# Projecting the memory's V 512 columns wide in a two-layer decoder trunk, with other fill pieces and another order of the cross-attention

## The chip, the core and the metric

The kernel runs on one core of a Trainium2 chip. Its time is the device time of one execution in microseconds; the time of a version is the median of several executions. TensorE multiplies matrices, ScalarE and VectorE evict and convert, GpSimd does some elementwise work, SyncE issues the transfers.

## What is computed

Two post-norm decoder layers on 256 tokens of width 1024, all in float32. Each layer has a token-mixing attention, a cross-attention into 256 memory tokens and a gated feed-forward part, each followed by a residual layer norm. The change touches the cross-attention:

```python
def memory_cross_attn(x, memn, wq, wkv, wo):
    q = (x @ wq).reshape(B, S, XA_HEADS, XA_DH)             # 4 heads of 256
    k, v = jnp.split(memn @ wkv, 2, axis=-1)
    s = jnp.einsum('bshd,bmhd->bhsm', q, k) * (XA_DH ** -0.5)
    p = jax.nn.softmax(s, axis=-1)
    o = jnp.einsum('bhsm,bmhd->bshd', p, v).reshape(B, S, XA_HEADS * XA_DH)
    return o @ wo
```

`memn` is the normed memory. It is the same for both layers and depends on no token, so K and V of a layer can be projected long before its cross-attention.

## The kernel before

**Products in three parts.** Each float32 operand is split into a high half (ScalarE copies it to the matmul's type) and a low half (VectorE subtracts), and a product is high x high, high x low and low x high, added up in one PSUM bank. Weights pass through `piece`: a load of up to 128 x 1024 into one of 4 raw buffers, then L130 (ScalarE, high) and L131 (VectorE, low) into one of 6 buffers each. `wmat` cuts a matrix into such pieces: four row blocks of 256 columns, or two of 512.

**Tokens.** There are two tiles of 128 tokens. After each norm `transposed` turns a tile with eight TensorE transposes into two banks, and ScalarE (L250) and VectorE (L251) evict the high and low half into `xT`. `mm_tr` (L177 to L179) has the weights stationary and streams both tiles, 256 columns; `mm_nat` (L169 to L171) has the tokens stationary and streams the weights' columns.

**Norms.** `layer_norm` takes a tile through VectorE (residual L217, mean L227), ScalarE (squares L228), VectorE (L229), GpSimd (reciprocal root L209) and VectorE again (L239, L240). The first tile's norm runs while TensorE still multiplies for the second.

**Fill pieces.** While the second tile's norm runs, TensorE gets work that wants no tokens: `fill(kv, n)` takes n pieces from `kv.work`, the four K pieces, and then from `kv.vwork`, the V pieces in the order `vord`. A K piece is 48 matmuls of 256 columns. A V piece before the change is a quarter of V's columns: 48 matmuls of 256 columns into one bank, first tile 0 of the memory, then tile 1. What V pieces are left when the cross-attention comes to them are projected there (`xa_v`) and split straight into the operand `vx`; those that were done as fill have been copied to a plain `kv.v` and are only split there.

For layer 0 three K pieces are placed by name in the attention's list of steps, and `lnfill` (3) pieces follow the first norm: K3, V1, V0. V2 and V3 are left to the cross-attention. For layer 1, `CFG[0]['fill']` (2) pieces stand behind the second norm of layer 0 (K0, K1), `CFG[1]['fill']` (2) behind the third norm of layer 0 (K2, K3), and `lnfill` (2) behind the first norm of layer 1 (V0, V1); V2 and V3 are left to the cross-attention.

**The order.** The program order of the steps is written out in two lists per layer, `attn` and `cross`. A list scheduler places the instructions on the engines by that order and by when it expects their inputs, so an engine may take a later step's instruction while an earlier one still waits. On the chip each engine then runs its instructions in the order so made. PSUM has eight banks in two pools of four, `a` and `b`; fill pieces and the accumulators of the output projections use pool `a`.

In the cross-attention's list, `q0` to `q3` project the queries, `qk0` to `qk3` make scores and softmax, `v0` to `v3` prepare V, and `av0` to `av3` transpose the probabilities and multiply them with V.

Of the kernel before, what the change touches and what calls it, by code (L numbers as in the profile page):

```python
# [13 lines left out]
AF = mybir.ActivationFunctionType  # L14
# [5 lines left out]
D = 1024  # L20
S = 256
DEPTH = 2
NT = S // P
KD = D // P
# [29 lines left out]
def consts():  # L54
# [24 lines left out]


CFG = [
    {'attn': 'kc nq1 nq0 par k cmp v mem tab qk0 cq qk1 cps ckv cmt fill av0 qk2 av1 av2 ch qk3 kr mq2 mq0 fill mkv par2 mq1 mq3 av3 mqk2 mqk3 mqk0 mqk1 mav0 mav1 fill mav3 mav2', 'cross': 'q2 q3 q0 q1 qk2 qk3 qk0 v0 v2 v1 qk1 av2 av0 v3 av1 av3', 'ev': [[[0, 0], [1, 0]], [1, 1]], 'fill': 2, 'lnfill': 3, 'vord': (1, 0, 3, 2), 'xt': ('q1', 'k1', 'q0'), 'opt': {'B': 0, 'M': 1, 'C': 0, 'N00': 0, 'N01': 0, 'N10': 0, 'N11': 0, 'N20': 0, 'N21': 0, 'R0': 1, 'R1': 1, 'K': 0, 'H': 0, 'X0': 0, 'X1': 1}, 'lnact': {'in': [0, 1], 'mem': [1, 0], '1': [1, 1], '2': [0, 0], '3': [0, 1]}, 'last': 5, 'natural': 0, 'bank': {'acc0': 'a', 'acc1': 'a', 'fill': 'a', 'proj': 'a', 'pv': 'a', 'mpv': 'b', 'mlav': 'b', 'xpv': 'b', 'nat': 'a', 'lnt': 'b', 'par': 'a', 'projt': 'a', 'cmp': 'b', 'cmps': 'b', 'cmpt': 'a', 'pt': 'b', 'qk': 'b', 'cht': 'a', 'mla': 'a', 'mqk': 'b', 'xq': 'a', 'xqk': 'a', 'xpt': 'b', 'up': 'b'}},
    {'attn': 'kc nq1 nq0 k cmp v qk0 cps ckv cmt av0 qk1 qk2 cq av1 ch av2 qk3 kr mq0 mkv mq3 mq1 av3 mqk0 mq2 mqk1 mqk3 mav0 mav3 mqk2 mav1 mav2', 'cross': 'q0 q1 q2 q3 qk0 v0 v2 av0 v1 qk1 qk2 qk3 v3 av2 av3 av1', 'ev': [[[0, 0], [0, 0]], [1, 1]], 'fill': 2, 'lnfill': 2, 'vord': (0, 1, 2, 3), 'xt': ('q1', 'k1', 'q0'), 'opt': {'B': 0, 'M': 1, 'C': 0, 'N00': 0, 'N01': 0, 'N10': 0, 'N11': 0, 'N20': 0, 'N21': 0, 'R0': 0, 'R1': 0, 'K': 0, 'H': 0, 'X0': 1, 'X1': 1}, 'lnact': {'in': [1, 1], 'mem': [1, 1], '1': [1, 1], '2': [0, 0], '3': [0, 0]}, 'last': 5, 'natural': 1, 'bank': {'acc0': 'a', 'acc1': 'a', 'fill': 'a', 'proj': 'a', 'pv': 'a', 'mpv': 'b', 'mlav': 'b', 'xpv': 'a', 'nat': 'a', 'lnt': 'b', 'par': 'b', 'projt': 'a', 'cmp': 'b', 'cmps': 'b', 'cmpt': 'a', 'pt': 'b', 'qk': 'b', 'cht': 'a', 'mla': 'a', 'mqk': 'a', 'xq': 'b', 'xqk': 'b', 'xpt': 'b', 'up': 'b'}},
]
SIZES = (4, 6, 6)
BUFS = {"a": 4, "b": 4}
# [3 lines left out]
def trunk(ctx: ExitStack, tc: tile.TileContext, a: dict, out: bass.AP):  # L90
    nc = tc.nc
    V, A, G, T = nc.vector, nc.scalar, nc.gpsimd, nc.tensor
# [10 lines left out]
    def bank(kind):  # L103
        tag = cfg['bank'][kind]
        return ps_.tile([P, 512], F32, name=kind, tag=tag, bufs=BUFS[tag])
# [11 lines left out]
    def piece(nk, n, segs, wn=None, cols=None):  # L117
        r = wp.tile([P, 1024], F32, name="raw", tag="raw", bufs=RAW)
        rv = r[:, :nk * n].rearrange("p (k n) -> p k n", k=nk)
        for krange, crange, src, *pr in segs:  # L120
            p0, p1 = pr[0] if pr else (0, P)
            nc.sync.dma_start(rv[p0:p1, krange[0]:krange[1], crange[0]:crange[1]], src)
        wn = wn or n
        h = wp.tile([P, 1024], F32R, name="hi", tag="hi", bufs=HL)
        lo = wp.tile([P, 1024], F32R, name="lo", tag="lo", bufs=HL)
        hv = h[:, :nk * wn].rearrange("p (k n) -> p k n", k=nk)
        lv = lo[:, :nk * wn].rearrange("p (k n) -> p k n", k=nk)
        for rs, ds in cols or [(lambda v: v, lambda v: v)]:
            x_, h_, l_ = rs(rv), ds(hv), ds(lv)
            A.activation(h_, x_, AF.Copy)  # L130
            V.tensor_tensor(l_, x_, h_.bitcast(F32), op=ALU.subtract)  # L131
        return hv, lv

    def wmat(w, cuts, ks=KD, cols=None, wn=None):

        n = sum(c1 - c0 for c0, c1 in cuts)
        per = max(1, 1024 // (wn or n))
        out_ = []
        for k0 in range(0, ks, per):
            k1 = min(ks, k0 + per)  # L140
            segs, o = [], 0
            for c0, c1 in cuts:
                segs.append(((0, k1 - k0), (o, o + c1 - c0),
                             w[k0 * P:k1 * P, c0:c1].rearrange("(k p) n -> p k n", p=P)))
                o += c1 - c0
            h, lo = piece(k1 - k0, n, segs, wn, cols)
            out_ += [(h[:, i], lo[:, i]) for i in range(k1 - k0)]
        return out_
# [13 lines left out]
    def split(hl, x):  # L162
        A.activation(hl[0], x, AF.Copy)
        V.tensor_tensor(hl[1], x, hl[0].bitcast(F32), op=ALU.subtract)

    def mm_nat(o, xh_, xl_, t, ws):

        for k, (h, lo) in enumerate(ws):
            T.matmul(o, xh_[:, t, k], h, start=k == 0, stop=False)  # L169
            T.matmul(o, xh_[:, t, k], lo, start=False, stop=False)  # L170
            T.matmul(o, xl_[:, t, k], h, start=False, stop=k == len(ws) - 1)  # L171

    def mm_tr(o, xh_, xl_, ws, m0):

        ms = slice(m0, m0 + P)
        for k, (h, lo) in enumerate(ws):
            T.matmul(o, h[:, ms], xh_[:, :, k], start=k == 0, stop=False)  # L177
            T.matmul(o, h[:, ms], xl_[:, :, k], start=False, stop=False)  # L178
            T.matmul(o, lo[:, ms], xh_[:, :, k], start=False, stop=k == len(ws) - 1)  # L179
# [103 lines left out]
    par = const.tile([P, NPAR], F32, name="par", tag="par")  # L283
# [46 lines left out]
    mh, ml = [big.tile([P, NT, KD, P], F32R, name="mT" + s, tag="mT" + s) for s in "hl"]  # L330
# [16 lines left out]
    def kv_work(l):  # L347
        kv = KV()
        kv.k = [big.tile([P, KD, S], F32R, name="xk" + s, tag="xk" + s) for s in "hl"]
        kv.v = big.tile([P, NT, D], F32, name="xv", tag="xv")  # L350
        w = a["xa_wkv"][l]

        def kpart(i):
            ws = wmat(w, [(i * 256, (i + 1) * 256)])
            pa = bank("fill")
            for m in range(2):
                mm_tr(pa[:, m * S:(m + 1) * S], mh, ml, ws, m * P)
            split([k[:, 2 * i:2 * i + 2, :] for k in kv.k], pa.rearrange("p (m n) -> p m n", m=2))

        def vpart(i, hl=None):  # L360
            ws = wmat(w, [(D + i * 256, D + (i + 1) * 256)])
            pa = bank("fill")
            for t in range(NT):
                mm_nat(pa[:, t * S:(t + 1) * S], mh, ml, t, ws)
            src = pa.rearrange("p (t n) -> p t n", t=NT)
            if hl is None:
                A.activation(kv.v[:, :, i * 256:(i + 1) * 256], src, AF.Copy)
            else:
                split(hl, src)

        kv.work = [lambda i=i: kpart(i) for i in range(4)]
        kv.vwork = {i: lambda *hl, i=i: vpart(i, *hl) for i in CFG[l]['vord']}
        return kv

    kvs = {}
# [20 lines left out]
    for l in range(DEPTH):  # L396
        cfg.update(CFG[l])
        w = a["w_in"][l]
        qs = [big.tile([P, 4, S], F32R, name=f"qs{g}", tag=f"q{g}") for g in range(2)]
        kk = [big.tile([P, 2, 2, S], F32R, name=f"kk{g}", tag=f"k{g}") for g in range(2)]  # L400
        kc = st.tile([P, 2, 2, 16], F32R, name="kc", tag="kc", bufs=1)
# [3 lines left out]
        kr = st.tile([P, NT, P], F32, name="kr", tag="kr", bufs=1)  # L405
# [379 lines left out]
        def mem():  # L785
# [3 lines left out]
        steps = {  # L789
            "kc": lambda: e.update(c2=in_kc()),  # L790
            "k": in_k,
            "v": in_v,
            "cq": in_cq,
            "ckv": in_ckv,
            "par": lambda: load_params((0,)),
            "par2": lambda: load_params((1, 2, 3)),
            "tab": load_tables,
# [50 lines left out]
        qx, vx, pTx = {}, [], []  # L848
# [35 lines left out]
        def xa_v(i):  # L884
            if not vx:
                v2 = big.tile([P, 2, NT, D], F32R, name="xv2", tag="xT")
                vx.extend([v2[:, 0], v2[:, 1]])
            v, *hl = [x[:, :, i * 256:(i + 1) * 256] for x in (kvs[l].v, *vx)]
            if i in kvs[l].vwork:
                kvs[l].vwork.pop(i)(hl)  # L890
            else:
                split(hl, v)

# [21 lines left out]
        steps = {}  # L915
        for i in range(4):
            steps[f"q{i}"] = lambda i=i: xa_q(i)
            steps[f"qk{i}"] = lambda i=i: xa_qk(i)
            steps[f"v{i}"] = lambda i=i: xa_v(i)
            steps[f"av{i}"] = lambda i=i: xa_av(i)  # L920
        for name in cfg['cross'].split():
            steps[name]()
# [139 lines left out]
```

## Time and profile before

| | |
|---|---|
| median of 3 runs | 880.95 us (879.26 to 881.2) |
| the profiled execution | 879.98 us |
| its span, first to last instruction | 877.9 us |
| mean granted TensorE clock | 0.993 of full speed |
| busy: TensorE, VectorE, ScalarE, GpSimd | 860.3, 665.2, 532.5, 132.4 us |

Busy time is the time in which an engine had at least one instruction under way. A matmul's duration includes the tail of the pipeline, so rows of TensorE overlap; the step between two starts is its pace.

### The profile page before, as it was taken

To read this page: it belongs to the slowest core of one execution; us is meant where nothing else is said; L and a number is where in the kernel's file an instruction comes from. 1 tells how busy PE (TensorE), PEld (TensorE's weight loads), DVE (VectorE), ACT (ScalarE), POOL (GpSimd) and SP (SyncE) were. 2 spreads that over 40 slices of the span, in tenths; PEclk is the share of its full clock that TensorE was granted. 3 is DMA by queue.
4 is the path that set the end of the run, shared out by engine and by line. 5 is a ranking of instruction groups with operands and counts; after the bars stand their busy time and mean duration, and the time that the engine had idled before them with its cause. 6 is when DMAs were issued, how large, how long until landed. Compare 5 with 4: busy or idle time off the path is not lost.

```text
span 877.9 us, 14948 instructions
## 1 busy us (share of the span) xinstructions
PE 860.3 (98%) x5502; PEld 766.7 (87%) x5502; DVE 665.2 (76%) x1290; ACT 532.5 (61%) x1014; POOL 132.4 (15%) x140
## 2 busy tenths in 40 slices
PE   8989999999999999999999999999999999999996
PEld 5989798899989888888989998879998888888895
DVE  7789887766578877677688788968566877777777
ACT  5658764555546676666555678636573567667661
POOL 1052000000000332222300020000000033223220
PEclk9989999999999999999999999999999999999998
DMA  7944463476347756656538634446633655665641
GB/s 229 284 145 124 132 173 113 140 251 190 96 123 237 217 158 216 190 165 217 183 110 239 190 90 110 144 127 210 194 119 121 218 159 179 212 192 171 215 142 48
DMA packets 128236, 148.66 MB, mean 169 GB/s; under 512 B 6259, under 2 KB 111009, under 8 KB 128163
## 3 DMA queue, kind: packets, MB, share of 16 engines
q1 hardware_dynamic: 128159, 147.70, 54.5%
q8 instruction: 43, 0.70, 0.3%
q14 instruction: 30, 0.25, 0.1%
q10 hardware_dynamic: 4, 0.01, 0.0%
HBM read 146.64 MB, written 1.05 MB: 168 GB/s over the span
## 4 chain that ended last, share of the span: by engine, by line
PE 91%; DVE 4%; ACT 2%; DMA 2%; issue 1%; POOL 0%; SPq 0%; DVEq 0%; ACTq 0%; POOLq 0%
PE up L259 16%; PE up L261 8%; PE acc L996 5%; PE acc L997 5%; PE acc L998 5%; PE acc L170 3%; PE acc L171 3%; PE acc L169 3%; PE fill L178 2%; PE fill L179 2%; PE xq L179 2%; PE xq L178 2%; PE xq L177 2%; PE fill L171 2%; PE fill L169 2%; PE fill L170 2%
## 5 line engine op out<-in xcount | busy, mean ns | idle before, releaser
L131 DVE TENSOR_TENSOR lo<-raw,hi 128x1024 fp32r<-128x1024 f32 (+5 forms) x296 | 322.8, 1108 | 96.2 <-ACT hi L130 94.0
L130 ACT ACTIVATE hi<-raw 128x1024 fp32r<-128x1024 f32 (+5 forms) x296 | 275.8, 951 | 108.9 <-PE acc L171 34.4
L259 PE MATMUL up<-xT,hi 128*128 128x512 f32 x608 | 152.1, 392 | 0.0
L259 PEld LDWEIGHTS up<-xT,hi 128*128 128x128 f32 x608 | 110.3, 189 | 20.3
L261 PEld LDWEIGHTS up<-xT,lo 128*128 128x128 f32 x608 | 82.9, 190 | 5.9
L984 POOL TENSOR_TENSOR cv<-cv 128x256 f32<-128x256 f32 x40 | 54.2, 1356 | 218.7 <-ACT cv L982 170.0
L261 PE MATMUL up<-xT,lo 128*128 128x256 f32 x608 | 84.8, 282 | 0.0
L978 ACT ACTIVATE cv<-u,par 128x256 f32<-128x256 f32 x76 | 45.4, 598 | 49.6 <-DVE u L971 49.6
L996 PE MATMUL acc<-hi,frh 128*128 128x512 f32 x176 | 68.9, 392 | 0.0
L997 PE MATMUL acc<-lo,frh 128*128 128x512 f32 x176 | 68.8, 391 | 0.0
L998 PE MATMUL acc<-hi,frl 128*128 128x512 f32 x176 | 68.2, 389 | 0.0
L209 POOL TENSOR_TENSOR mv<-mv,mhalf 128x1 f32<-128x1 f32 x16 | 14.3, 897 | 309.0 <-DVE mv L233 158.5
L979 DVE SCALAR_TENSOR_TENSOR cv<-u,par,cv 128x255 f32<-128x255 f32 x76 | 37.6, 495 | 26.4 <-ACT cv L978 26.4
L584 ACT ACTIVATE p<-p,nm 128x128 f32<-128x128 f32 x96 | 42.6, 447 | 9.7 <-DVE nm L581 9.4
L986 ACT ACTIVATE frh<-cv 128x256 fp32r<-128x256 f32 x44 | 18.4, 418 | 37.8 <-POOL cv L984 35.4
L987 POOL TENSOR_TENSOR frl<-cv,frh 128x256 fp32r<-128x256 f32 x40 | 38.0, 952 | 20.3 <-ACT frh L986 20.3
L980 DVE SCALAR_TENSOR_TENSOR cv<-u,par,cv 128x254 f32<-128x254 f32 x76 | 37.9, 498 | 2.5
L998 PEld LDWEIGHTS acc<-hi,frl 128*128 128x128 f32 x176 | 33.0, 188 | 7.5 <-DVE frl L987 0.7
L996 PEld LDWEIGHTS acc<-hi,frh 128*128 128x128 f32 x176 | 33.1, 188 | 7.0 <-ACT frh L986 0.9
L997 PEld LDWEIGHTS acc<-lo,frh 128*128 128x128 f32 x176 | 33.1, 188 | 6.0
L177 PE MATMUL fill<-mTh,hi 128*128 128x256 f32 x128 | 37.2, 291 | 0.0
L179 PE MATMUL fill<-mTh,lo 128*128 128x256 f32 x128 | 36.6, 286 | 0.0
(279 smaller groups left out, 2151.7 us busy)
## 6 DMA issues: line engine op xcount, KB each, us to landing
raw<-in_ffn_w_up SPq DMA_DIRECT2D x88, 512.0 KB, 4.4
raw<-in_ffn_w_down SPq DMA_DIRECT2D x44, 512.0 KB, 4.3
raw<-in_xa_wkv SPq DMA_DIRECT2D x32, 512.0 KB, 3.8
raw<-in_xa_wq SPq DMA_DIRECT2D x16, 512.0 KB, 5.4
raw<-in_xa_wo SPq DMA_DIRECT2D x16, 512.0 KB, 4.2
raw<-in_w_in SPq DMA_DIRECT2D x24, 256.0 KB, 3.4
raw<-in_w_out SPq DMA_DIRECT2D x16, 256.0 KB, 4.6
raw<-in_w_out SPq DMA_DIRECT2D x8, 512.0 KB
```

What stands on the lines that cost most here:

```text
L130: A.activation(h_, x_, AF.Copy)
L131: V.tensor_tensor(l_, x_, h_.bitcast(F32), op=ALU.subtract)
L169: T.matmul(o, xh_[:, t, k], h, start=k == 0, stop=False)
L177: T.matmul(o, h[:, ms], xh_[:, :, k], start=k == 0, stop=False)
L179: T.matmul(o, lo[:, ms], xh_[:, :, k], start=False, stop=k == len(ws) - 1)
L259: T.matmul(o, h[:, ms], x2[:, k], start=k == 0, stop=False)
L261: T.matmul(o[:, 0:S], lo[:, ms], x2[:, k, 0], start=False, stop=k == len(ws) - 1)
L978: A.activation(c, u, AF.Identity, bias=pcol("cb", l, ft), scale=w_[2])
L984: E.tensor_tensor(conv[0], conv[0], conv[1], op=ALU.mult)
L996: T.matmul(o, fh[:, ts_], h[:, cs_], start=f == 0, stop=False)
L997: T.matmul(o, fh[:, ts_], lo[:, cs_], start=False, stop=False)
L998: T.matmul(o, fl[:, ts_], h[:, cs_], start=False, stop=f == NF - 1)
```

## The change

V is projected in two pieces of 512 columns instead of four of 256. A piece takes two banks, one for each tile of the memory, and goes through the row blocks once, with both tiles at each block; each tile is evicted by itself. The steps `v2` and `v3` fall away. The counts of fill pieces become smaller, and the cross-attention's steps get another order:

| | before | after |
|---|---|---|
| layer 0, behind the first norm (`lnfill`) | 3: K3, V1, V0 (256 wide) | 2: K3, V0 (512 wide) |
| layer 1, behind the third norm of layer 0 (`CFG[1]['fill']`) | 2: K2, K3 | 1: K2 |
| layer 1, behind its first norm (`lnfill`) | 2: V0, V1 | 1: K3 |
| layer 1, projected in the cross-attention | V2, V3 | V0, V1, which are all of V |
| layer 0, `cross` | q2 q3 q0 q1 qk2 qk3 qk0 v0 v2 v1 qk1 av2 av0 v3 av1 av3 | q2 q3 q0 q1 qk2 qk3 qk0 v0 qk1 v1 av2 av0 av1 av3 |
| layer 1, `cross` | q0 q1 q2 q3 qk0 v0 v2 av0 v1 qk1 qk2 qk3 v3 av2 av3 av1 | q0 q1 q2 q3 qk0 qk1 v0 av0 qk2 qk3 v1 av1 av2 av3 |

`vord` becomes (0, 1) in both layers. All other entries of the two configurations stay.

```diff
         def vpart(i, hl=None):
-            ws = wmat(w, [(D + i * 256, D + (i + 1) * 256)])
-            pa = bank("fill")
-            for t in range(NT):
-                mm_nat(pa[:, t * S:(t + 1) * S], mh, ml, t, ws)
-            src = pa.rearrange("p (t n) -> p t n", t=NT)
-            if hl is None:
-                A.activation(kv.v[:, :, i * 256:(i + 1) * 256], src, AF.Copy)
-            else:
-                split(hl, src)
+
+            ws = wmat(w, [(D + i * 512, D + (i + 1) * 512)])
+            pa = [bank("fill") for _ in range(NT)]
+            for k, (h, lo) in enumerate(ws):
+                for t in range(NT):
+                    T.matmul(pa[t], mh[:, t, k], h, start=k == 0, stop=False)
+                    T.matmul(pa[t], mh[:, t, k], lo, start=False, stop=False)
+                    T.matmul(pa[t], ml[:, t, k], h, start=False, stop=k == KD - 1)
+            for t in range(NT):
+                if hl is None:
+                    A.activation(kv.v[:, t, i * 512:(i + 1) * 512], pa[t], AF.Copy)
+                else:
+                    split([x[:, t, i * 512:(i + 1) * 512] for x in hl], pa[t])
...
-            v, *hl = [x[:, :, i * 256:(i + 1) * 256] for x in (kvs[l].v, *vx)]
+            v, *hl = [x[:, :, i * 512:(i + 1) * 512] for x in (kvs[l].v, *vx)]
             if i in kvs[l].vwork:
-                kvs[l].vwork.pop(i)(hl)
+                kvs[l].vwork.pop(i)(vx)
             else:
                 split(hl, v)
...
-            steps[f"v{i}"] = lambda i=i: xa_v(i)
+            if i < 2:
+                steps[f"v{i}"] = lambda i=i: xa_v(i)
```

## Rows read from the trace of the kernel before

**Rows 1.** The page's busy time by engine, share of the span, instructions.

```profile
PE 860.3 (98%) x5502; PEld 766.7 (87%) x5502; DVE 665.2 (76%) x1290; ACT 532.5 (61%) x1014; POOL 132.4 (15%) x140
```

**Rows 2.** Busy time by stretch, with instructions, granted clock and transfers.

```profile
core 0: us, PE busy (x) PEld busy (x) DVE busy (x) ACT busy (x) POOL busy (x), PEclk, DMA share, GB/s
...
445.00:470.00 25.00, 25.00 (x165) 22.32 (x164) 22.30 (x41) 12.86 (x21) 2.50 (x3) 1.00 0.46 132
...
585.00:606.00 21.00, 21.00 (x127) 18.62 (x125) 16.51 (x27) 12.50 (x16) 2.01 (x2) 1.00 0.56 173
606.00:680.00 74.00, 73.88 (x534) 69.91 (x534) 45.24 (x59) 38.68 (x63) 0.99 (x1) 1.00 0.51 165
```

**Rows 3.** TensorE's timeline (start us, us, ...): 47 output-projection matmuls, 47 of a K piece.

```profile
156.28 0.39 PE L171 MATMUL acc<-hi,oTl 128*128 128x512 f32 x1
...
166.71 0.39 PE L169 MATMUL acc<-hi,oTh 128*128 128x512 f32 x1
...
171.10 0.28 PE L178 MATMUL fill<-mTl,hi 128*128 128x256 f32 x1
...
176.62 0.28 PE L179 MATMUL fill<-mTh,lo 128*128 128x256 f32 x1
```

**Rows 4.** The last eviction behind layer 0's first norm, and the first query matmul.

```profile
181.65 0.68 DVE L251 TENSOR_TENSOR xT<-lnt,xT 128x512 fp32r<-128x512 f32 x1
...
189.34 0.28 PE L177 MATMUL xq<-xT,hi 128*128 128x256 f32 x1
```

**Rows 5.** TensorE's timeline behind layer 1's first norm.

```profile
598.38 0.36 PE L169 MATMUL fill<-hi,mTh 128*128 128x256 f32 x1
...
606.09 0.63 PE L247 MATMUL lnt<-c_ident,x 128*128 128x128 f32 x4
...
611.06 0.28 PE L177 MATMUL xq<-xT,hi 128*128 128x256 f32 x1
```

**Rows 6.** VectorE's and ScalarE's timelines in the same stretch.

```profile
601.54 2.35 DVE L131 TENSOR_TENSOR lo<-raw,hi 128x1024 fp32r<-128x1024 f32 x2
...
606.52 1.22 DVE L131 TENSOR_TENSOR lo<-raw,hi 128x1024 fp32r<-128x1024 f32 x1
607.66 1.28 DVE L251 TENSOR_TENSOR xT<-lnt,xT 128x512 fp32r<-128x512 f32 x2
...
606.75 1.27 ACT L250 ACTIVATE xT<-lnt 128x512 fp32r<-128x512 f32 x2 [0.79 <-PE lnt L247]
```

**Rows 7.** TensorE's timeline behind layer 0's third norm.

```profile
457.11 0.36 PE L177 MATMUL fill<-mTh,hi 128*128 128x256 f32 x1
...
464.27 0.60 PE L247 MATMUL lnt<-c_ident,x 128*128 128x128 f32 x4
...
469.57 0.40 PE L487 MATMUL projt<-xT,hi 128*128 128x256 f32 x2
```

**Rows 8.** ScalarE's timeline in the same stretch.

```profile
465.07 1.15 ACT L130 ACTIVATE hi<-raw 128x512 fp32r<-128x512 f32 x2 [0.30 <-DMA raw<-in_w_in]
466.13 1.06 ACT L250 ACTIVATE xT<-lnt 128x512 fp32r<-128x512 f32 x2
```

**Rows 9.** Layer 1's last V piece and the first product after it: TensorE, ScalarE.

```profile
653.47 1.25 PE L899 MATMUL xpt<-c_ident,xp 128*128 128x128 f32 x10
654.81 0.39 PE L909 MATMUL xpv<-pTx,xv 128*128 128x256 f32 x1
...
653.67 0.60 ACT L163 ACTIVATE xv<-fill 128x512 fp32r<-128x512 f32 x1 [0.38 <-PE fill L171]
```

**Rows 10.** Layer 0's compression: a wait of TensorE, and the stretches around it.

```profile
50.77 0.64 PE L523 MATMUL cmp<-c_ident,hs 34*128 34x34 f32 x4 [3.18 <-DVE hs L160]
...
47.00:51.00 4.00, 0.82 (x7) 0.59 (x6) 3.91 (x7) 3.36 (x5) 4.00 (x5) 0.83 0.84 264
51.00:55.00 4.00, 4.00 (x19) 3.93 (x19) 4.00 (x13) 2.71 (x6) 3.88 (x3) 0.50 0.84 236
55.00:60.00 5.00, 5.00 (x35) 5.00 (x35) 2.78 (x9) 3.21 (x10) 1.34 (x3) 0.85 0.14 48
```

More of the change, by code (lines that the diff above doesn't have):

```diff
@@ L81 @@
 CFG = [
-    {'attn': 'kc nq1 nq0 par k cmp v mem tab qk0 cq qk1 cps ckv cmt fill av0 qk2 av1 av2 ch qk3 kr mq2 mq0 fill mkv par2 mq1 mq3 av3 mqk2 mqk3 mqk0 mqk1 mav0 mav1 fill mav3 mav2', 'cross': 'q2 q3 q0 q1 qk2 qk3 qk0 v0 v2 v1 qk1 av2 av0 v3 av1 av3', 'ev': [[[0, 0], [1, 0]], [1, 1]], 'fill': 2, 'lnfill': 3, 'vord': (1, 0, 3, 2), 'xt': ('q1', 'k1', 'q0'), 'opt': {'B': 0, 'M': 1, 'C': 0, 'N00': 0, 'N01': 0, 'N10': 0, 'N11': 0, 'N20': 0, 'N21': 0, 'R0': 1, 'R1': 1, 'K': 0, 'H': 0, 'X0': 0, 'X1': 1}, 'lnact': {'in': [0, 1], 'mem': [1, 0], '1': [1, 1], '2': [0, 0], '3': [0, 1]}, 'last': 5, 'natural': 0, 'bank': {'acc0': 'a', 'acc1': 'a', 'fill': 'a', 'proj': 'a', 'pv': 'a', 'mpv': 'b', 'mlav': 'b', 'xpv': 'b', 'nat': 'a', 'lnt': 'b', 'par': 'a', 'projt': 'a', 'cmp': 'b', 'cmps': 'b', 'cmpt': 'a', 'pt': 'b', 'qk': 'b', 'cht': 'a', 'mla': 'a', 'mqk': 'b', 'xq': 'a', 'xqk': 'a', 'xpt': 'b', 'up': 'b'}},
@@ L83 @@
-    {'attn': 'kc nq1 nq0 k cmp v qk0 cps ckv cmt av0 qk1 qk2 cq av1 ch av2 qk3 kr mq0 mkv mq3 mq1 av3 mqk0 mq2 mqk1 mqk3 mav0 mav3 mqk2 mav1 mav2', 'cross': 'q0 q1 q2 q3 qk0 v0 v2 av0 v1 qk1 qk2 qk3 v3 av2 av3 av1', 'ev': [[[0, 0], [0, 0]], [1, 1]], 'fill': 2, 'lnfill': 2, 'vord': (0, 1, 2, 3), 'xt': ('q1', 'k1', 'q0'), 'opt': {'B': 0, 'M': 1, 'C': 0, 'N00': 0, 'N01': 0, 'N10': 0, 'N11': 0, 'N20': 0, 'N21': 0, 'R0': 0, 'R1': 0, 'K': 0, 'H': 0, 'X0': 1, 'X1': 1}, 'lnact': {'in': [1, 1], 'mem': [1, 1], '1': [1, 1], '2': [0, 0], '3': [0, 0]}, 'last': 5, 'natural': 1, 'bank': {'acc0': 'a', 'acc1': 'a', 'fill': 'a', 'proj': 'a', 'pv': 'a', 'mpv': 'b', 'mlav': 'b', 'xpv': 'a', 'nat': 'a', 'lnt': 'b', 'par': 'b', 'projt': 'a', 'cmp': 'b', 'cmps': 'b', 'cmpt': 'a', 'pt': 'b', 'qk': 'b', 'cht': 'a', 'mla': 'a', 'mqk': 'a', 'xq': 'b', 'xqk': 'b', 'xpt': 'b', 'up': 'b'}},
+    {'attn': 'kc nq1 nq0 par k cmp v mem tab qk0 cq qk1 cps ckv cmt fill av0 qk2 av1 av2 ch qk3 kr mq2 mq0 fill mkv par2 mq1 mq3 av3 mqk2 mqk3 mqk0 mqk1 mav0 mav1 fill mav3 mav2', 'cross': 'q2 q3 q0 q1 qk2 qk3 qk0 v0 qk1 v1 av2 av0 av1 av3', 'ev': [[[0, 0], [1, 0]], [1, 1]], 'fill': 2, 'lnfill': 2, 'vord': (0, 1), 'xt': ('q1', 'k1', 'q0'), 'opt': {'B': 0, 'M': 1, 'C': 0, 'N00': 0, 'N01': 0, 'N10': 0, 'N11': 0, 'N20': 0, 'N21': 0, 'R0': 1, 'R1': 1, 'K': 0, 'H': 0, 'X0': 0, 'X1': 1}, 'lnact': {'in': [0, 1], 'mem': [1, 0], '1': [1, 1], '2': [0, 0], '3': [0, 1]}, 'last': 5, 'natural': 0, 'bank': {'acc0': 'a', 'acc1': 'a', 'fill': 'a', 'proj': 'a', 'pv': 'a', 'mpv': 'b', 'mlav': 'b', 'xpv': 'b', 'nat': 'a', 'lnt': 'b', 'par': 'a', 'projt': 'a', 'cmp': 'b', 'cmps': 'b', 'cmpt': 'a', 'pt': 'b', 'qk': 'b', 'cht': 'a', 'mla': 'a', 'mqk': 'b', 'xq': 'a', 'xqk': 'a', 'xpt': 'b', 'up': 'b'}},
@@ new lines @@
+    {'attn': 'kc nq1 nq0 k cmp v qk0 cps ckv cmt av0 qk1 qk2 cq av1 ch av2 qk3 kr mq0 mkv mq3 mq1 av3 mqk0 mq2 mqk1 mqk3 mav0 mav3 mqk2 mav1 mav2', 'cross': 'q0 q1 q2 q3 qk0 qk1 v0 av0 qk2 qk3 v1 av1 av2 av3', 'ev': [[[0, 0], [0, 0]], [1, 1]], 'fill': 1, 'lnfill': 1, 'vord': (0, 1), 'xt': ('q1', 'k1', 'q0'), 'opt': {'B': 0, 'M': 1, 'C': 0, 'N00': 0, 'N01': 0, 'N10': 0, 'N11': 0, 'N20': 0, 'N21': 0, 'R0': 0, 'R1': 0, 'K': 0, 'H': 0, 'X0': 1, 'X1': 1}, 'lnact': {'in': [1, 1], 'mem': [1, 1], '1': [1, 1], '2': [0, 0], '3': [0, 0]}, 'last': 5, 'natural': 1, 'bank': {'acc0': 'a', 'acc1': 'a', 'fill': 'a', 'proj': 'a', 'pv': 'a', 'mpv': 'b', 'mlav': 'b', 'xpv': 'a', 'nat': 'a', 'lnt': 'b', 'par': 'b', 'projt': 'a', 'cmp': 'b', 'cmps': 'b', 'cmpt': 'a', 'pt': 'b', 'qk': 'b', 'cht': 'a', 'mla': 'a', 'mqk': 'a', 'xq': 'b', 'xqk': 'b', 'xpt': 'b', 'up': 'b'}},
```

## The prediction

> **What bounds the kernel now.** I read the page first. TensorE is busy 860.3 of 877.9 us, so only two things can move the end: fewer microseconds of TensorE work, or new waits of TensorE [rows 1]. Then the table by stage, to see whether that holds where the change is. It does: TensorE has no idle time behind the third norm of layer 0, none around the first norm of layer 1, and 0.12 of 74 us in that layer's cross-attention; the clock is 1.00 throughout. VectorE is busy 22.3 of 25 us behind the third norm, so the norm chain there shares a crowded engine [rows 2]. Then TensorE's timeline, for the real pace: a row's duration there includes the pipeline's tail, so the price of a matmul is the step from one start to the next. Last, the timelines of ScalarE and VectorE behind the norms, to see when the transposed tokens are ready, and what the fill pieces cover until then.
>
> **The streams.** The change replaces, in each layer, 4 pieces of 48 matmuls of 256 columns by 2 pieces of 48 of 512. From 171.10 to 176.62 there are 46 steps: 0.120 us each. From 156.28 to 166.71 there are 46 steps of 512 columns: 0.2267 us each [rows 3]. A layer's V was 192 x 0.120 = 23.04 us and becomes 96 x 0.2267 = 21.76 us, which saves 1.28 us, over two layers 2.55 us. These matmuls lie end to end, so this gain is real time unless waits eat it. Rounding of the two paces moves it by less than 0.2 us.
>
> The rows say that a matmul costs its columns at 2.4 GHz (106.7 and 213.3 ns) and 13 ns more, and the 13 ns is what widening saves [rows 3]. The Trainium skill (TensorE: Matmul & The Clock Gate, "Back-to-back issue gap") gives columns/2.4 and 2.5 ns more, which speaks against widening: 192 matmuls fewer would save 0.48 us only, and the sum below would end 2.1 us later. The trace does not agree with that figure.
>
> Evictions cost nothing on the path: a 256-wide piece had one 128x512 eviction for both tiles, a 512-wide one has two, so there are as many per layer as before; in layer 1 two copies to the plain V and their later splits fall away. ScalarE and VectorE have room for all this (busy 38.7 and 45.2 of 74 us in that cross-attention) [rows 2]. Loads stay at 16 of 512 KB per layer, on the same queue, in longer runs; I price that at nothing either.
>
> **Where the cover goes.** In layer 0 three pieces behind the first norm become one K piece (5.76 us) and one wide V piece (10.88 us): 16.64 us against 17.28. The last eviction that the queries need ends at 181.65 + 0.68 = 182.3 us, and the queries began at 189.34 [rows 4]; some 6 us of cover stay. Price: nothing. The wide piece needs two banks at once, but the K piece stands ahead of it, and the accumulators are released meanwhile.
>
> Layer 1 is different. The pieces are taken in the order K0 to K3, then V. Before, K2 and K3 stood behind the third norm of layer 0, V0 and V1 behind the first norm of layer 1: 96 matmuls, 11.5 us, at each. Afterwards only K2 stands at the one and K3 at the other: 48 matmuls, 5.76 us. What is removed is done in the cross-attention instead, and is priced above, so it is no saving here: if TensorE could go on at once, everything behind it would come 5.76 us earlier, and what it comes later than that is a new stall.
>
> First norm of layer 1: fill started at 598.38. 48 matmuls end at about 604.1. The second tile's transposes start at 606.09, and the queries started at 611.06 [rows 5]. Their inputs: the high half's evictions run from 606.75, the low half's from 607.66 to 608.9 [rows 6]. The first query matmul wants the high half of four blocks (about 607.4), its second the low half (608.3). Without any stall the queries would start at 611.06 - 5.76 = 605.3. So the stall is 607.4 - 605.3 = 2.1 us at least and 608.3 - 605.3 = 3.0 us at most. I take 2.8, since the query's three products go block by block and the second one needs the low half.
>
> Third norm of layer 0: fill started at 457.11, so K2 ends at 462.9; the transposes start at 464.27; the compressed branch's projection started at 469.57 [rows 7], without a stall it would at 463.8. It begins with all its products of the high half, so only ScalarE's two evictions matter. They stood at 466.13, behind two weight conversions at 465.07 [rows 8]. In front of those the first would be done at about 465.6, behind them at 466.8: a stall of 1.8 to 3.0 us. I take 2.3. Behind that projection are queued the whole input projections, all in TensorE's order, so nothing later recovers it.
>
> Neither place has other work to offer: the next weights' high and low halves have six buffers, and the removed piece's two go to the projections that wait for the same tile.
>
> **The cross-attention's steps.** After the last V piece TensorE now runs four heads in a row. Before, in layer 1, it ran ten transposes behind the last V piece and then came to the first product at 654.81, 1.34 us after the first transpose: that product needs the probabilities, which ScalarE evicts only after V (0.60 us at 653.67) [rows 9]. A wide piece has a second eviction of 0.60 us in front of the probabilities. Lower bound nothing (the transposes were placed earlier), upper bound those 0.60 us and a quarter more for latency, 0.75 us, per layer. I take 0.4 each, 0.8 together. The query steps ahead of it keep their order, and the scores that are moved ahead of V (qk1) have their softmax behind 10.9 us of V.
>
> **Sum.** 879.98 (span 877.9 and 2.1 around it) - 2.55 + 2.3 + 2.8 + 0.8 = 883.3 us. The profiled execution was 0.97 us under the median of the runs shown, 880.95; by that one it is 884.3. I say 883.8. The bounds give -2.55 + 1.8 + 2.1 + 0 = +1.35 and -2.55 + 3.0 + 3.0 + 1.5 = +4.95, so this case's own range is 881.3 to 885.9.
>
> **Rivals.**
>
> *The chain behind the norms gets shorter (faster).* VectorE's own steps of the second tile were held up by splits of weights: two of them (2.35 us from 601.54) between the mean and the variance, one of 1.22 us at 606.52 in front of the last evictions [rows 6]. With one piece fewer its splits might not stand there. If the tile is ready 2.5 us earlier at both places, 0.3 us is left of the two stalls; without one in the cross-attentions the result is 879.98 - 2.55 + 0.3 = 877.7, by the median 878.7. For it: VectorE is nearly full there. Against it: the buffers let the next weights in at once, so as many splits are ready to step in. It decides for faster when all new stalls together stay under 0.8 us. Chance 0.26.
>
> *Half of it.* One of the two places finds cover (products of the first tile alone, or V's, which want no tokens) or each stalls half as long: -2.55 + 2.6 + 0.8 = +0.85, 881.8 by the median: no measurable change. Chance 0.22.
>
> *The clock falls as well.* TensorE waited 3.18 us before 50.77, and the mean granted clock was 0.83 in that stretch of 4 us, 0.50 in the next 4 and 0.85 in 5 more [rows 10]: 1.4 + 4 + 1.5 = 6.9 us at 1.2 GHz, which cost up to half of that, 3.4 us. Behind the first norm of layer 1 there would be some 4 us with only eight transposes in them. The Trainium skill (TensorE: Matmul & The Clock Gate, "Why this matters for your kernels") warns of idle gaps between bursts, and this stretch agrees. Then 884.3 + 3.4 = 887.7. Against it: the transposes break the gap. Chance 0.13.
>
> **How the numbers follow.** The forecast has 0.39. Measurements tell 0.2%, 1.8 us, from no change. Faster is the first rival: 0.26. The second and the lower end of the forecast make no change: 0.24. The rest of the forecast and the clock make slower: 0.50. As cases of both signs hold most of the chance, the range reaches from under the first rival to the last one: 878.2 to 888.0; what lies outside has at most 0.2.
>
> **What the new profile would show.** The saving: V's matmuls 512 wide at 0.227 us, 192 fewer in all, TensorE's busy time down. The stalls: idle time of TensorE before the second tile's transposes and before the first xq in layer 1 (2 to 3 us), and before the first projt (about 2 us), both put down to evictions or to VectorE's norm steps. If those waits are missing, the cover was not needed and the prediction is wrong on the fast side; if the granted clock shows 0.50 there, on the slow side.

## The result, and the profile after

The changed kernel takes 886.23 us (median of 4 executions, 885.32 to 887.24) against 880.11 for the kernel before (4 executions, 878.17 to 881.20): 1.0072 times, 95% interval 1.0049 to 1.0095. It is slower, by 6.1 us, where 2.85 was forecast (883.8 beside 880.95). Here and below a ratio is an estimate from all executions of both kernels, so it is not quite the quotient of the two medians. The profiled execution took 886.14 us, its span is 883.9 us, 6.0 more than before.

The page's busy time, engine by engine, answers to [rows 1]:

```profile
PE 860.8 (97%) x5310; PEld 757.2 (86%) x5310; DVE 666.5 (75%) x1289; ACT 531.2 (60%) x1011; POOL 132.0 (15%) x140
```

There are 192 matmuls fewer, as planned, and yet TensorE's busy time did not fall (860.8 after 860.3), while its share did: it now waits. To see where, I divided both spans at the same events, the start of the first tile's transposes behind each norm (L247). The four stretches run from layer 0's first norm to its second, to its third, to layer 1's first norm, and to layer 1's second. First the kernel before, then the changed one; the columns are those of [rows 2].

```profile
170.11:259.35 89.24, 89.21 (x657) 84.80 (x656) 59.37 (x80) 46.73 (x71) 2.50 (x3) 1.00 0.52 166
259.35:456.20 196.85, 196.85 (x1113) 172.32 (x1112) 152.45 (x228) 125.08 (x204) 48.12 (x42) 1.00 0.60 190
456.20:597.59 141.39, 140.00 (x991) 125.12 (x990) 115.38 (x327) 93.64 (x230) 8.53 (x13) 1.00 0.51 145
597.59:681.23 83.64, 83.52 (x610) 79.12 (x609) 54.88 (x73) 45.62 (x72) 1.98 (x2) 1.00 0.51 164
```

```profile
168.37:259.44 91.07, 88.36 (x562) 79.56 (x561) 59.37 (x79) 46.53 (x70) 2.49 (x3) 1.00 0.52 162
259.44:456.32 196.88, 196.88 (x1113) 172.31 (x1112) 152.50 (x228) 125.12 (x204) 48.08 (x42) 1.00 0.60 190
456.32:593.86 137.54, 134.87 (x943) 119.36 (x942) 112.67 (x324) 91.32 (x227) 8.52 (x13) 1.00 0.50 141
593.86:687.29 93.43, 90.48 (x561) 81.16 (x560) 58.76 (x76) 46.97 (x73) 1.97 (x2) 0.98 0.49 158
```

The stretch of layer 0's cross-attention is 1.83 us longer although it lost 1.28 us of work: TensorE is busy 88.36 of 91.07 us where it was busy 89.21 of 89.24. The feed-forward part, which the change doesn't touch, is equal. The stretch of the third norm is 3.85 us shorter, but a K piece of 5.76 us has left it: 1.9 us of new waits. That of layer 1's first norm and cross-attention is 9.79 us longer: 5.76 for the K piece that came, 1.28 less for the width, and 5.3 of new waits and of a lower clock (0.98). What follows it is equal to 0.1 us. The last term has nothing to do with the change: layer 0's first norm comes 1.74 us earlier (168.37 after 170.11), with the same instructions ahead of it, on each engine in the same order. It is told of at the end.

The places, in TensorE's timeline of the changed kernel (start, duration, then what ran; in brackets the idle time before it and its releaser): V's last products, the first heads and the first product of the output projection (`acc`) in layer 0, then the third norm, then layer 1's first norm. The second and third answer to [rows 7] and [rows 5].

```profile
216.13 0.39 PE L368 MATMUL fill<-hi,mTl 128*128 128x512 f32 x1
...
226.34 0.39 PE L368 MATMUL fill<-hi,mTl 128*128 128x512 f32 x1
226.57 0.60 PE L903 MATMUL xpt<-c_ident,xp 128*128 128x128 f32 x4
228.82 0.38 PE L913 MATMUL xpv<-pTx,xv 128*128 128x256 f32 x1 [1.65 <-ACT pTx L163]
...
232.02 0.39 PE L913 MATMUL xpv<-pTx,xv 128*128 128x256 f32 x1 [1.06 <-ACT pTx L163]
...
235.91 0.48 PE L169 MATMUL acc<-hi,xoh 128*128 128x512 f32 x1
...
462.92 0.28 PE L179 MATMUL fill<-mTh,lo 128*128 128x256 f32 x1
464.12 1.32 PE L247 MATMUL lnt<-c_ident,x 128*128 128x128 f32 x8 [0.92 <-DVE x L240]
...
600.37 0.28 PE L179 MATMUL fill<-mTh,lo 128*128 128x256 f32 x1
602.36 1.29 PE L247 MATMUL lnt<-c_ident,x 128*128 128x128 f32 x8 [1.72 <-DVE x L240]
...
604.78 0.41 PE L179 MATMUL xq<-xT,lo 128*128 128x256 f32 x1
604.99 0.41 PE L177 MATMUL xq<-xT,hi 128*128 128x256 f32 x1
```

The wide products keep their pace: 45 steps in 10.21 us, 0.227 us each. Behind them come two waits, 1.65 and 1.06 us, both for the eviction of transposed probabilities. Behind both norms the fill piece ends before the second tile's norm does (`x` of L240), as forecast. After layer 1's first norm something more is to be seen: from 604.78 two starts of 256 columns are 0.21 us apart, not 0.12. The windows there give the clock that was granted (last columns but two):

```profile
600.40:604.00 3.60, 1.82 (x13) 1.20 (x11) 3.42 (x6) 2.45 (x4) 0.90 (x1) 0.99 0.87 268
604.00:608.00 4.00, 3.90 (x21) 3.60 (x20) 3.28 (x4) 0.29 (x1) 0.00 (x0) 0.59 0.91 303
608.00:612.00 4.00, 4.00 (x35) 4.00 (x35) 0.81 (x1) 1.52 (x2) 0.00 (x0) 1.00 0.67 243
```

TensorE was busy half of the first of them. In the next, 0.59 is a mix of the two levels: 0.41 x 4 us x 2 = 3.3 us at 1.2 GHz instead of 2.4, in which 1.6 to 1.7 us of work is lost. It stays busy, so this loss appears in no list of waits.

### The profile page after: what moved, and what is told of

It is laid out like the page before. It is cut to its first block, busy times and chain, and to the rows that moved or that the text cites. A ratio compares the mean times of both kernels' runs of the same rounds, so it can differ in the third digit from the quotient of the medians.

```text
span 883.9 us, 14559 instructions
## 1 busy us (share of the span) xinstructions
PE 860.8 (97%) x5310; PEld 757.2 (86%) x5310; DVE 666.5 (75%) x1289; ACT 531.2 (60%) x1011; POOL 132.0 (15%) x140
## 4 chain that ended last, share of the span: by engine, by line
PE 87%; DVE 5%; ACT 3%; DMA 2%; issue 1%; POOL 0%; SPq 0%; DVEq 0%; ACTq 0%; POOLq 0%
PE up L259 16%; PE up L261 8%; PE acc L1001 4%; PE acc L1002 4%; PE acc L1003 4%; PE acc L169 3%; PE acc L170 3%; PE acc L171 3%; DMA raw<-in_w_in 2%; PE xq L178 2%; PE xq L179 2%; PE xq L177 2%; PE pt L601 2%; PE fill L368 2%; PE fill L366 2%; PE fill L367 2%
## 5 line engine op out<-in xcount | busy, mean ns | idle before, releaser
L178 PE MATMUL xq<-xT,hi 128*128 128x256 f32 x128 | 37.0, 289 | 0.1
```

## The experiments

Theory: the width saves its 2.55 us; the two norms lose cover and cost some 6 us (2.3 at the third norm, 4.0 at layer 1's first), of which 1.7 are the clock; in the cross-attentions the order of steps, not the width of V, causes the new waits, because ScalarE takes other work ahead of the evictions that TensorE waits for. Rivals: the wide pieces themselves cause the waits (two evictions instead of one, two banks); or the lost cover alone does, and the cross-attentions' waits follow from it. Each ratio is against executions of the kernel before that were measured alongside (medians 879.96 for the first four, 879.59 for the next four, 881.53 for the last three); stretches are those of the table above.

**Cover behind layer 1's first norm.** `lnfill` of layer 1 from 1 to 2, so that K3 and V's first half stand there:

```diff
-'fill': 1, 'lnfill': 1
+'fill': 1, 'lnfill': 2
```

> Layer 1's lnfill goes from 1 to 2: K3 and the wide V0 stand behind its first norm, the third norm of layer 0 keeps K2 alone. Waits theory: TensorE's 1.9 us before the second tile's transposes, the small waits at the first query matmuls and the stretch at half clock behind them go, some 4.0 us: about 882.2 us beside 886.2 of the changed kernel. Wide-pieces theory (the wide pieces and their two banks are themselves slow): moving one wide piece changes nothing, within 1 us of the changed kernel.

Measured: 887.56 us, 1.0080 (1.0067 to 1.0094), no better than the changed kernel. The wait at the norm is gone, and the clock there is 1.00. But TensorE now waits in layer 1's cross-attention, and the clock falls behind that. The waits of TensorE from 590 to 690 us (in all, times, longest), and the windows at the first of them, the longer one:

```profile
PE xpt L903 <- ACT xp L152: 2.2, 1, 2.2
PE xpv L913 <- ACT pTx L163: 1.0, 1, 1.0
```

```profile
640.00:644.00 4.00, 1.80 (x16) 1.60 (x15) 3.43 (x6) 3.37 (x12) 0.00 (x0) 1.00 0.71 243
644.00:648.00 4.00, 4.00 (x23) 4.00 (x22) 1.55 (x3) 1.49 (x5) 0.00 (x0) 0.57 0.07 24
```

The V half that is done early is only split in the step `v0`, with no matmul in it. It was the 10.9 us in which the softmax of heads 0 and 1 was hidden. One V piece can cover one thing: taken to the norm, it lays the softmax bare. The stall moved. (4.0 us less had been expected.)

**Cover behind both norms.** K3 back behind the third norm and V's first half behind layer 1's first norm:

```diff
-'fill': 1, 'lnfill': 1
+'fill': 2, 'lnfill': 1
```

> Layer 1's counts become 2 and 1: K2 and K3 behind the third norm of layer 0, the wide V0 behind layer 1's first norm. Waits theory: both stalls go, 2.3 and 4.0 us, so about 879.9 us, even with the kernel before. Wide-pieces theory: no change from 886.2. If only the first norm's stall counts, 882.2.

Measured: 883.57 us, 1.0049 (1.0033 to 1.0065). The third norm's stretch is 141.50 us, as long as before; with the K piece of 5.76 us the changed kernel would have had 143.30, so the lost cover there was worth 1.8 us. Layer 1's stretch is 86.05 us where the width alone would give 83.64 - 1.28 = 82.36; the list of waits has the same two rows as the kernel above, 2.2 and 1.0 us. Layer 0 keeps its 91.10. So with both norms covered what remains of the loss is in the cross-attentions, and the 879.9 us expected are missed by 3.7. In layer 0 the waits owe nothing to the lost cover, and the second rival falls; in layer 1 the 2.2 us are new, from the V piece taken away.

One thing differs from the kernel above. TensorE waits 2.2 us before the same transposes, and yet the clock stays at 1.00 behind the wait, where it was 0.57:

```profile
638.00:642.00 4.00, 2.12 (x16) 1.94 (x17) 2.62 (x6) 3.56 (x13) 0.00 (x0) 1.00 0.61 199
642.00:646.00 4.00, 4.00 (x31) 3.83 (x31) 2.31 (x5) 2.50 (x8) 0.00 (x0) 1.00 0.00 0
```

So much the same wait, before the same transposes, is followed by a lower clock in one profile and not in the other.

**The order in layer 0 alone.** Head 0's product goes between `v0` and `qk1`:

```diff
-'q2 q3 q0 q1 qk2 qk3 qk0 v0 qk1 v1 av2 av0 av1 av3'
+'q2 q3 q0 q1 qk2 qk3 qk0 v0 av0 qk1 v1 av2 av1 av3'
```

> Only layer 0's cross-attention order is changed: head 0's av0 comes right after v0, before qk1 and v1; then av2 av1 av3. Theory of the probability buffers (head 1's exponentials wait for a buffer that head 2's transposes give back, and sit on ScalarE ahead of the evictions that TensorE waits for): av0 gives the buffers back before v1, head 1's exponentials run under v1, and the 1.8 us wait and the 1.2 us wait behind v1 shrink to about 1 us in all: 884 us. Rival, the second V eviction alone holds up the heads behind v1: the waits stay at about 3 us, 886.

Measured: the stretch falls from 91.07 to 87.97 us, 3.1 us, which is 1.27 under the kernel before, the width's saving; the list of TensorE's waits in that cross-attention is empty. One part of the cause can be read in ScalarE's timelines. First the changed kernel, then this one:

```profile
226.09 1.28 ACT L163 ACTIVATE xv<-fill 128x512 fp32r<-128x512 f32 x2 [0.98 <-PE fill L368]
227.26 0.47 ACT L883 ACTIVATE xp<-xqk,xm 128x256 f32<-128x256 f32 x1
...
227.71 0.47 ACT L883 ACTIVATE xp<-xqk,xm 128x256 f32<-128x256 f32 x1
...
228.16 0.60 ACT L163 ACTIVATE pTx<-xpt 128x512 fp32r<-128x512 f32 x1
```

```profile
222.43 0.58 ACT L163 ACTIVATE pTx<-xpt 128x512 fp32r<-128x512 f32 x1
222.91 0.47 ACT L883 ACTIVATE xp<-xqk,xm 128x256 f32<-128x256 f32 x1
...
223.36 0.48 ACT L883 ACTIVATE xp<-xqk,xm 128x256 f32<-128x256 f32 x1
...
230.96 1.29 ACT L163 ACTIVATE xv<-fill 128x512 fp32r<-128x512 f32 x2 [0.98 <-PE fill L368]
232.15 0.59 ACT L163 ACTIVATE pTx<-xpt 128x512 fp32r<-128x512 f32 x1
```

There are six buffers `xp` for probabilities, two per head, so three heads fill them: 2, 3 and 0. The exponentials of head 1 (L883) must wait until a head's probabilities have been transposed. In the changed order no transpose stands ahead of the second V piece, so they come after it, and on ScalarE they stand between V's evictions and the eviction `pTx`, on which TensorE waits. With `av0` ahead of `qk1` two buffers come free early, and the exponentials run while TensorE still multiplies for V.

That is the smaller part. From the transposes behind V to the first product it took 2.25 us (226.57 to 228.82), and takes 1.37 here: 0.9 less, the time of the two exponentials. The other part is in TensorE's timeline of this kernel:

```profile
231.45 0.60 PE L903 MATMUL xpt<-c_ident,xp 128*128 128x128 f32 x4
231.81 0.48 PE L169 MATMUL acc<-hi,xoh 128*128 128x512 f32 x1
...
232.82 0.36 PE L913 MATMUL xpv<-pTx,xv 128*128 128x256 f32 x1
```

Head 0 is finished before V's second piece ends, so products of the output projection are free to run while ScalarE evicts: four of them fill the 1.0 us from 231.81 to 232.82, and more of them the place of the second wait. In the changed kernel no head is finished by then, and the first such product runs only at 235.91. Its second wait, 1.06 us, has no exponential ahead of the eviction at all: on ScalarE `pTx` stands there behind the eviction of the first head's output. By these rows some 0.9 of the 3.1 us are the exponentials and the rest is the output projection as cover. That is an estimate, as no run takes the two apart.

The whole time fell by less: 885.37 us, 1.0061 (1.0049 to 1.0073). In the profiled execution layer 0's first norm came at 171.22 us, 2.85 later than in the changed kernel, which takes back nearly all of the 3.1: the early fall of the clock that is told of at the end lasted 6.8 us in it, not 3.4.

**The narrow products in the changed kernel.** Same banks, evictions and orders, but each product 256 columns wide:

```diff
-for k, (h, lo) in enumerate(ws):
-    for t in range(NT):
-        T.matmul(pa[t], mh[:, t, k], h, start=k == 0, stop=False)
...
+for t in range(NT):
+    for c in range(2):
+        cs_ = slice(c * 256, (c + 1) * 256)
+        mm_nat(pa[t][:, cs_], mh, ml, t, [(h[:, cs_], lo[:, cs_]) for h, lo in ws])
```

> The changed kernel with V's matmuls 256 columns wide again, two halves of a bank one after the other, with the same pieces, counts and order of steps. Pace theory (0.120 and 0.2267 us): 192 matmuls more, 2.55 us slower than the changed kernel, 888.8. By a fixed cost of 2.5 ns per matmul it would be 0.5 us slower, 886.7. Wide-pieces theory: faster than the changed kernel.

Measured: 891.09 us, 1.0126 (1.0111 to 1.0140), 4.9 us above the changed kernel. More than the width's 2.55: behind layer 0's waits the clock falls as well here, to a mean of 0.58 from 232 to 236 us. So this kernel does not isolate the width; the next pair does.

**Cover and order together.** The changed kernel with the cover of the second experiment, and scores and products taken by turns so that no head's softmax waits for buffers or for V. In both layers:

```diff
-'q2 q3 q0 q1 qk2 qk3 qk0 v0 qk1 v1 av2 av0 av1 av3'
-'q0 q1 q2 q3 qk0 qk1 v0 av0 qk2 qk3 v1 av1 av2 av3'
+'q0 q1 qk0 q2 qk1 q3 qk2 v0 av0 qk3 av1 v1 av2 av3'
...
-'fill': 1, 'lnfill': 1
+'fill': 2, 'lnfill': 1
```

> V wide as in the changed kernel, the fill counts of layer 1 at 2 and 1 (K2 and K3 behind the third norm, V0 behind the first), and in both layers the order q0 q1 qk0 q2 qk1 q3 qk2 v0 av0 qk3 av1 v1 av2 av3: each head's softmax has a query projection over it, and after the last V piece the output projection's first blocks are free to run. Waits theory: no new stall, the width's 2.55 us stay: about 877.5 us beside 880.0 of the kernel before. Wide-pieces theory: not under the kernel before.

and the same with the narrow products of the fourth experiment:

> The same counts and order as f1, with V's matmuls 256 columns wide, half a bank after the other: the width by itself where no stall stands beside it. Pace theory: 2.55 us slower than f1, about 880. By a fixed cost of 2.5 ns per matmul: 0.5 us slower.

Measured: wide 878.53 us, 0.9985 (0.9972 to 0.9997); narrow 882.07 us, 1.0024 (1.0011 to 1.0037): 3.5 us apart. Layer 0's stretch, which in both is free of listed waits above 0.1 us, wide and then narrow:

```profile
170.61:258.63 88.02, 88.02 (x561) 79.37 (x560) 59.79 (x79) 46.88 (x70) 2.50 (x3) 1.00 0.53 168
```

```profile
168.76:258.10 89.34, 89.31 (x658) 84.70 (x657) 59.08 (x79) 46.22 (x70) 2.63 (x3) 1.00 0.52 166
```

The width is worth 1.32 us in layer 0, where 1.28 was worked out. (In layer 1 the stretches are 83.78 and 85.85 us; 0.7 of that difference is a longer wait of the narrow kernel for `pTx`, 1.1 us after 0.4.) Over the four stretches the wide kernel is 1.3 us shorter than the kernel before, 88.02 + 196.90 + 141.11 + 83.78 after 511.12: the 2.6 of the width, less some waits that are left. Those in layer 1:

```profile
PE xqk L876 <- DVE qx L866: 0.8, 1, 0.8
...
PE xpv L913 <- ACT pTx L163: 0.4, 1, 0.4
```

The wide piece does not cause the waits: the first rival falls too.

**The lost cover alone.** The kernel before, with narrow V and its own orders, but with one fill piece at each of the two norms:

```diff
-'fill': 2, 'lnfill': 2
+'fill': 1, 'lnfill': 1
```

> The kernel before with layer 1's two counts lowered to 1 and 1 and nothing else: V narrow, all four V pieces in the cross-attention, its order kept. Waits theory: the third norm's stall (2.3 us) and the first norm's (2.3 us and 1.7 of half clock) appear in the narrow kernel as well: 884 to 886 us. Wide-pieces theory: no change from 880.

Measured: 888.09 us, 1.0084 (1.0066 to 1.0102). No new wait in the cross-attentions, but both norms wait, and in the profiled execution the clock falls at both; the waits there and the windows:

```profile
PE lnt L247 <- DVE x L240: 2.6, 2, 1.7
PE projt L487 <- ACT xT L250: 1.0, 1, 1.0
```

```profile
462.00:466.00 4.00, 3.04 (x23) 2.36 (x21) 3.54 (x7) 1.84 (x4) 1.51 (x2) 1.00 0.91 244
466.00:471.00 5.00, 4.04 (x21) 4.04 (x22) 4.69 (x9) 2.95 (x6) 0.00 (x0) 0.66 0.18 41
602.00:606.00 4.00, 2.25 (x17) 1.71 (x16) 3.95 (x7) 2.71 (x4) 0.99 (x1) 1.00 0.75 237
606.00:611.00 5.00, 4.75 (x25) 4.47 (x25) 3.67 (x5) 0.65 (x2) 0.00 (x0) 0.66 0.87 284
```

The two stretches give 139.43 - (141.39 - 5.76) = 3.8 and 93.60 - (83.64 + 5.76) = 4.2 us. Fewer pieces alone, without any wide one, cost 8.0 us by the stretches and 8.5 by the medians. Two of the six executions, with mean clocks of 0.994 and 0.996, took 885.0 and 884.8 us, the other four, with 0.990 and 0.991, from 887.8 to 888.8.

**Is the fall of the clock an effect of the wait?** Fourteen matmuls of 256 columns into a bank that nobody reads, added to the changed kernel behind the fill of layer 1's first norm. The first attempt used the transposes' kind of bank (`lnt`), the second that of the fill pieces:

```diff
+if l == 1:
+    pw = bank("fill")
+    for i in range(14):
+        T.matmul(pw[:, 0:S], mh[:, 0, 0], mh[:, 0, 0:2], start=i == 0, stop=i == 13)
```

> The changed kernel with 14 matmuls of no use (1.7 us) between K3 and the second tile's transposes of layer 1, where TensorE waits; they write a bank that nobody reads. If the half clock behind that wait comes from TensorE's idle time, it goes and 1.7 us with it: 884.5 beside 886.2; the wait itself stays. If not, nothing changes, or the work delays the transposes and it gets slower.

> f4 with its 14 idle-filling matmuls (1.7 us, into a fill bank that nobody reads) in front of the second tile's transposes of layer 1 instead of behind them. TensorE's wait there shrinks to 0.2 us. If the half clock behind the wait came from the idle time, the clock stays at 1.00 and the time is 1.7 us under the changed kernel, 884.5. If it came from elsewhere, 886.2.

The first came out at 887.45 us, 1.0078 (1.0062 to 1.0094), and tells nothing: the matmuls were scheduled behind the transposes, which still waited 1.71 us, and the clock still fell (0.58 from 604 to 608 us). In the second they fill the gap, and the transposes follow without a wait; TensorE's timeline and the windows:

```profile
603.60 1.84 PE L853 MATMUL fill<-mTh 128*128 128x256 f32 x14
605.47 1.29 PE L247 MATMUL lnt<-c_ident,x 128*128 128x128 f32 x8
```

```profile
604.00:608.00 4.00, 3.69 (x27) 2.86 (x26) 3.88 (x6) 2.74 (x4) 0.41 (x1) 1.00 0.88 291
608.00:612.00 4.00, 4.00 (x36) 4.00 (x35) 2.38 (x3) 0.07 (x1) 0.00 (x0) 1.00 0.78 279
```

The clock stays at 2.4 GHz. The queries come no earlier for this work, but run at full pace: the stretch falls from 93.43 to 92.15 us, by 1.28, and the time to 886.50 us, 1.0058 (1.0046 to 1.0070) against 1.0072. The two intervals overlap, so the gain is read from the stretch and the clock, not from the totals. The other profiles agree on this place: in all six with a wait of 1.71 or 1.72 us before these transposes the clock falls behind it, and in the seven without that wait it doesn't.

**The orders alone, and a better order for layer 1.** The changed kernel with the new orders of the pair above but with its own fill counts; and the wide one of that pair with this order in layer 1, where `av0` and `av1` come earlier:

```diff
-'q0 q1 qk0 q2 qk1 q3 qk2 v0 av0 qk3 av1 v1 av2 av3'
+'q0 q1 qk0 q2 qk1 q3 v0 av0 qk2 av1 qk3 v1 av2 av3'
```

> The changed kernel with f1's order of the cross-attention in both layers and its own fill counts (1 and 1): the two norms' stalls stay (2.3 us, 2.3 us and 1.7 of half clock), the cross-attentions' new ones go (3.2 us in layer 0, 0.8 to 1.3 in layer 1): 4 to 4.5 us under the changed kernel, about 882. If the cross-attention's order were innocent: 886.2.

> f1 with another order in layer 1's cross-attention: q0 q1 qk0 q2 qk1 q3 v0 av0 qk2 av1 qk3 v1 av2 av3, so that no scores stand right behind the query projection whose low half they need. In f1 TensorE waited 0.9 us there and 0.6 us behind the last V piece; the first wait should go: about 0.9 us under f1, some 2 us under the kernel before. If the wait only moves to the first product with V, no change from f1.

Measured: the orders alone 884.97 us, 1.0040 (1.0027 to 1.0052), that is 2.8 us below the changed kernel by the two ratios; layer 0's stretch is 88.08 us, 3.0 less, layer 1's 93.10, 0.3 less where 0.8 to 1.3 was expected, with the wait at its first norm and the half clock behind it still there. The other takes 878.60 us, 0.9968 (0.9956 to 0.9979), against 0.9985 with the first of the new orders. Both beat the changed kernel and the kernel before. Which of the two is better is not told by that: their medians are 878.5 and 878.6, and it is the kernel before that differs between the two sets of executions (879.59 and 881.53). By the stretches the second order does what it was meant to in layer 1, here behind that of the third norm:

```profile
453.71:596.23 142.52, 140.67 (x991) 125.15 (x990) 115.20 (x327) 93.33 (x230) 8.53 (x13) 1.00 0.50 144
596.23:679.49 83.26, 82.38 (x514) 73.89 (x513) 55.22 (x72) 45.46 (x71) 1.98 (x2) 1.00 0.53 165
```

Layer 1's is 83.26 us instead of 83.78, but the stretch before it takes 1.4 us more than with the first order (142.5 after 141.1). The engines run the same instructions there in the same order. What differs is that ScalarE waited 1.94 us instead of 0.57 for a load of `in_w_out`, and VectorE and TensorE came late behind it; why the load was late was not followed up.

## Why the prediction was right, and where its sizes were off

It was right in the direction, and the time lies in its range, but 0.3 us above the 885.9 at which the forecast's own bounds ended. The range reached to 888.0 for the sake of the clock rival. The clock did fall, but the largest excess, 3.6 us in the two cross-attentions, belongs to no rival, so that the time came out inside the range is in part luck. Term by term, against the profiled execution before:

| term | forecast (bounds) | measured | from |
|---|---|---|---|
| width of V, both layers | -2.55 | -2.6 | layer 0's stretch, wide and narrow: 1.32, taken twice |
| third norm of layer 0 | +2.3 (1.8 to 3.0) | +1.9 | its stretch; 1.8 when the cover is put back |
| first norm of layer 1 | +2.8 (2.1 to 3.0) | +4.0 | its last query starts 4.0 us late: 1.7 of half clock, 2.3 of waits |
| cross-attention, layer 0 | +0.4 (0 to 0.75) | +3.1 | its stretch, with the order undone |
| cross-attention, layer 1 | +0.4 (0 to 0.75) | +1.3 | the rest of layer 1's stretch |
| before layer 0's first norm | 0 | -1.7 | not the change's |
| sum | +3.35 | +6.0 | the spans: 883.9 - 877.9 |

*The width* was priced rightly, by the step between two starts. The figure of the Trainium skill (TensorE: Matmul & The Clock Gate, "Back-to-back issue gap"), which it gives for the isolated gap of a matmul, would by estimate have given 0.24 us a layer; the trace does not agree, with 1.32.

*The norms.* Layer 0's first norm was rightly priced at nothing: from 168 to 262 us TensorE's list of waits has the cross-attention's rows alone. At layer 0's third norm and layer 1's first the mechanism was right: the fill piece ends, TensorE waits for VectorE's last norm step, then for the evictions. The rival that VectorE would finish earlier for lack of splits did not come about: the transposes waited for it 0.92 and 1.72 us. What was mis-sized is layer 1: the wait was 2.3 us, inside the bounds worked out, but the clock fell behind it. That was held for a rival of its own with a chance of 0.13, against which it was said that the transposes break the gap; they did not prevent it. The rival's price of 3.4 us was twice too high: the half clock lasted 3.4 us here, not 6.9, and cost half of that. The second kernel with added matmuls shows that the clock stays up at this place when the idle time is filled. The Trainium skill (TensorE: Matmul & The Clock Gate, "Why this matters for your kernels") warns of idle gaps between bursts; the 1.72 us here is shorter than the gaps it names, and the measurement decides.

*The cross-attentions* are the term that failed. The step said that "the scores that are moved ahead of V (qk1) have their softmax behind 10.9 us of V", and its upper bound counted only a second eviction of V, 0.60 us and a quarter for latency. But the scores' exponentials need a free pair of the six probability buffers, and the steps that free them had been moved behind V. So two exponentials, 0.9 us, joined V's evictions ahead of the eviction that TensorE wanted. And TensorE had nothing to run meanwhile: before, V's last narrow piece stood between the products and products of the output projection behind it, but now no head was finished when V was. The step had taken its rows from layer 1 alone and left out what covers an eviction. Undoing one step of the order gave all 3.1 us back. That layer 1's 1.3 us have the same cause was not tried by itself: there the new order alone gave 0.3 us back, and cover and order together left 1.2 of listed waits in that stretch. Its one listed wait in the changed kernel, 1.0 us, has no exponential ahead of its eviction, so there the cause stays open.

Where the expected gain went is thus accounted for: the width's 2.6 us are there, and 10.3 us of new waits and half clock stand against them. Of these 9.1 do not belong to the width: with other counts and another order the same wide pieces run the four stretches in 509.8 us instead of 518.9. The other 1.2 were not removed by any run.

## What to carry to other kernels

When a piece of independent work is moved, ask at both ends what it had covered: the same 10.9 us of V hid a norm in one place and a softmax in the other, and could be spent only once. Before a step is moved ahead, count the buffers that it writes and find the step that frees them; if that one lies behind the long work, the moved step does too, and can land in front of an eviction that the critical engine wants. Ask also what the critical engine can run during that eviction: one head finished early frees the output projection for it. And price a new wait of TensorE of a microsecond or two with the chance of a lower clock behind it: where that came it added 1.3 to 1.7 us, and it shows only in the granted clock.

## What the runs showed of the hardware that was not expected

A wait of 1.72 us, followed by eight transposes and query matmuls with small waits between them, was followed by about 3.4 us at 1.2 GHz; in the third norm of the same kernel, with waits of 0.92 and 0.68 us, the clock stayed at 2.4 GHz. The length of a wait does not settle it: with fewer pieces in the kernel before, the clock fell behind waits of 0.92 and 1.0 us at that norm, and with V's first half behind layer 1's norm it stayed up there behind 0.92 and 1.5 us; and one wait of 2.2 us was followed by a fall in one kernel and by none in another. Which waits lower the clock was not mapped further.

Early in the program, long before anything that the change touches, the clock falls as in [rows 10], and for how long differs between executions. The windows of the changed kernel there:

```profile
47.00:51.00 4.00, 1.70 (x15) 1.43 (x14) 3.63 (x6) 3.17 (x6) 3.94 (x5) 0.99 0.74 218
51.00:55.00 4.00, 4.00 (x21) 4.00 (x21) 4.00 (x16) 2.53 (x7) 3.37 (x4) 0.58 0.84 264
```

0.42 x 4 us x 2 = 3.4 us at 1.2 GHz, where the kernel before had 6.9. In the thirteen profiled executions it was 3.4 us in six and 6.8 to 6.9 in seven. This is the 1.7 us by which the changed kernel was ahead at layer 0's first norm, and by which the comparison of the two profiled executions flatters the change. In the wide kernel with cover and order repaired, the two executions with a mean clock of 0.999 took 875.8 and 876.1 us, the four with 0.993 and 0.994 from 879.0 to 880.1. Why the length differs stays open; no experiment was made on it.
